# A transformer block in split fp32: q, k and dv scratch with one stride per partition and spilled by ScalarE, modulation sums in PSUM, part of the FFN modulation loaded later

## The chip, the core and the metric

The kernel runs on one core of a Trainium2 chip. A core has a matmul engine (TensorE, PE in the profile, with its weight loads as PEld), three engines for elementwise work (VectorE or DVE, ScalarE or ACT, GpSimd or POOL), a fifth that here only issues DMAs (SyncE or SP), and 16 DMA engines that all queues share. Each engine works through its own list of instructions in order and waits on semaphores for the others. The metric is the device time of one execution in microseconds (us); less is better.

## The reference, cut to what matters

One block of a transformer on S = 1024 tokens of width D = 1024, batch 1, depth 1, in float32. A vector `c` modulates both halves of the block through six vectors of 1024 numbers:

```python
c_act = jax.nn.silu(c)
mod = c_act @ w_ada[l] + b_ada[l]                    # [1, 6144]
sh_a, sc_a, g_a, sh_f, sc_f, g_f = jnp.split(mod[:, None, :], 6, axis=-1)
h = rms_norm(x, g_mix[l]) * (1.0 + sc_a) + sh_a
x = x + g_a * hybrid_mixer(h, w_in[l], ...)
h = rms_norm(x, g_ffn[l]) * (1.0 + sc_f) + sh_f
x = x + g_f * swiglu(h, w_ffn_gate[l], w_ffn_up[l], w_ffn_down[l])
return rms_norm(x, g_final)
```

The mixer multiplies `h` by `w_in` (1024 x 2240) and splits the result into `dq` and `dk` (4 heads of 2 x 64 features each), `dv` (4 x 128), `q_lat` (384), `kv_lat` (256) and `k_rope` (64). Four heads are differential attention (two softmaxes with a linear position bias, the second subtracted with a factor lambda), four are latent attention (`q_lat` and `kv_lat` normalised, multiplied up, rotated). Both are causal. Then comes the output projection, and a gated FFN of width 2816.

The six sections of `w_ada` (4 MB each) have the numbers 0 to 5 in the kernel: 0 and 1 (`sh_a`, `sc_a`) are needed before the first matmul of the block, 2 (`g_a`) at the output projection, 3 and 4 (`sh_f`, `sc_f`) at the second norm, 5 (`g_f`) where the FFN's down projection is scaled.

## The kernel before

**Numbers in two parts.** Every fp32 matrix is split into a high and a low part (`split`, L151 and L155: a rounded copy, by ScalarE as a rule, then the difference, by VectorE or GpSimd), and each product is three matmuls (`mm3`, L370 to L372: high by high, high by low, low by high).

**Memory.** All large tiles come from one pool of 49 slots of 4 KB per partition. PSUM has two double banks (`psd`) and four single ones (`psb`). What does not fit goes to scratch in DRAM and comes back (`scr_q`, `scr_k`, `scr_dv`, `scr_mv` and others). SyncE issues all loads (`ld`), GpSimd all spills (`sd`).

**Order.** The code is written as one list of steps, and a scheduler lays the instructions out for each engine from it; instructions marked `pin` keep their place in the written order. `Stream` (L58 to L95) holds the loads with their preparation. `add` appends a pair (DMA, preparation), `allow` sets how far the stream may run, `need` runs it up to a named item, `pump(n)` runs n preparations, and loads are issued up to `ahead` items in front of the preparations. `defer(n, fn)` puts a spill off by n calls of `tick()`.

**Stages.** After the first loads comes

1. `g1(0)`, then `g1(1)` (L414): for one half of the tokens, `dq` and `dk`, transposed (features on the partitions). For each of 8 row tiles k of `w_in`, `make_h` (L353) transposes the normalised x by four matmuls against the identity (L356), ScalarE scales it by the modulation columns into a tile `ht` (L361), and `split` makes `hh` and `hl`. Six outputs are accumulated over k while k runs, two more afterwards. `evac_qk` (L397) splits each of the 8 outputs into a tile E, [128, 2 (high, low), 512], and spills it.
2. During `g1(0)`, `ada_cols(k)` (L217) makes the columns of sections 0 and 1 for row tile k: 8 multiply-add steps on VectorE over weight rows (256 wide, two running sums in SBUF, added at the end), then two matmuls by ones (L229), which add over the partitions, and two small operations into `acol`.
3. `dv` for 8 tiles of 128 tokens (`evac_v`, L463), then `lat_q`, `lat_k` and their up projections mixed with the first attention steps ("fill", with `PUMP` preparations and `ALLOW` limits after each piece), then the rest of the attention steps (`step`), the output projection, the FFN chunk by chunk, and the down projection.

**Sections 2 to 5.** `ada_items(sec, ...)` (L264) adds 8 stream items for a section: each loads 512 KB (`adr`) and adds it, times one number per partition, to a sum `acc` [128, 1024] on VectorE (L275 for the first, L277 for the other seven, each depending on the one before). Three ticks later `row_bc` (L287; sections 2 and 5) makes it a row on all partitions by two pinned matmuls and two additions, or `col_sec` (L305; sections 3 and 4) makes it columns by eight pinned matmuls 1 wide. The stream's order is: 8 pairs of ada and `w_in` tiles, x tiles 4 to 7, section 2, section 4, `w_in` for dv, `w_in` for lat_q, section 3, section 5, `w_in` for lat_k, rope, the two up projections. So all four sections are done before lat_q.

**Scratch.** `scr_q` and `scr_k` are [head, half, P, 2, 512], with row l*64 + r for the high (l = 0) or low (l = 1) part of feature r, and 2 for the softmax m. A spill of an E is two DMAs of 256 KB by GpSimd, one each for the high and the low part (L404). `load_t` (L712) reads for each step A (the high half of q, twice, into the two halves of the partitions), Q (the low half, the same) and K (all of k, one DMA). dv is spilled as four DMAs of 256 KB for each two tiles of tokens, in pieces of 512 bytes (L472).

Of the kernel before, what the change touches and what calls it, by code (L numbers as in the profile page):

```python
# [24 lines left out]
ALLOW = [(6, 'rope'), (15, ('qup', 2)), (25, ('kvup', 1)), (34, None)]  # L25
# [4 lines left out]
PUMP = (2, 2)  # L30
# [66 lines left out]
def emit(ctx, tc, a, out, dbg=None, rec=None):  # L97
# [112 lines left out]

    def load_ada(k):
        adar[k] = [slot([4, 256], F32, "ada") for _ in range(2)]
        for q in range(2):
            ld(out=adar[k][q], in_=a["ada_a"][k, :, q * 4:(q + 1) * 4, :])

    def ada_cols(k):
        acc = slot([2, 256], F32, "acc")  # L217
        for kt in range(8):
            src = adar[k][kt // 4][:, kt % 4, :]
            c = cact[:, kt:kt + 1]  # L220
            if kt < 2:
                nc.vector.tensor_scalar(out=acc[:, kt, :], in0=src, scalar1=c, scalar2=None, op0=ALU.mult)
            else:
                nc.vector.scalar_tensor_tensor(out=acc[:, kt % 2, :], in0=src, scalar=c, in1=acc[:, kt % 2, :],
                                               op0=ALU.mult, op1=ALU.add)
        nc.vector.tensor_tensor(out=acc[:, 0, :], in0=acc[:, 0, :], in1=acc[:, 1, :], op=ALU.add)
        ps = psb()
        for s in range(2):
            mm(ps[:, s:s + 1], lhsT=acc[:, 0, s * 128:(s + 1) * 128], rhs=ones[:, 0:1], start=True, stop=True)  # L229
        nc.vector.scalar_tensor_tensor(out=acol[:, 0, k:k + 1], in0=ps[:, 0:1], scalar=b1col(1, k),  # L230
                                       in1=V[:, 56 + k:57 + k], op0=ALU.add, op1=ALU.mult)
        nc.vector.tensor_tensor(out=acol[:, 1, k:k + 1], in0=ps[:, 1:2], in1=bcol(0, k), op=ALU.add)
        del adar[k]
# [17 lines left out]
    load_ada(0)  # L251
    for t in range(4):
        load_x(t)
    st = Stream(3)
    win = a["w_in"]
    for k in range(8):
        st.add(("ada", k), (lambda k=k: load_ada(k)) if k else (lambda: None), lambda k=k: ada_cols(k))
        witem(st, ("s0", k), win[k * P:(k + 1) * P, 0:1024], [1024], nc.gpsimd)
# [5 lines left out]
    def ada_items(sec, done):  # L264
        for kt in range(8):
# [17 lines left out]
            st.add(("ad", sec, kt), dma, prep)  # L283
# [3 lines left out]
    def row_bc(sec):  # L287
# [3 lines left out]

        st.add(("gb", sec), dma, lambda: None)
# [10 lines left out]
        ada_items(sec, done)  # L303

    def col_sec(sec, fin):  # L305
        def done(acc):
            ps = psb()
            for j in range(8):
                pin(mm(ps[:, j:j + 1], lhsT=acc[:, j * 128:(j + 1) * 128], rhs=ones[:, 0:1], start=True, stop=True))
            fin(ps)  # L310

        ada_items(sec, done)
# [7 lines left out]

    row_bc(2)
    col_sec(4, fin_scf)
    for q in range(4):
        witem(st, ("dv", q), win[q * 256:(q + 1) * 256, 1024:1536].rearrange("(k p) n -> p k n", p=P), [2, 512], nc.gpsimd)
    for q in range(4):
        witem(st, ("lq", q), win[q * 256:(q + 1) * 256, 1536:1920].rearrange("(k p) n -> p k n", p=P), [2, 384])
    col_sec(3, fin_shf)
    row_bc(5)

# [3 lines left out]

    for q in range(3):
        n = 3 if q < 2 else 2
        witem(st, ("lk", q), win[q * 384:q * 384 + n * 128, 1920:2240].rearrange("(k p) n -> p k n", p=P), [n, 320])
# [3 lines left out]
    for k in range(2):  # L340
        witem(st, ("kvup", k), a["w_kv_up"][k * P:(k + 1) * P, :], [1024], nc.gpsimd)

# [10 lines left out]
    def make_h(hf, k):  # L353
# [6 lines left out]
        tmp = slot([512], F32, "ht")  # L360
        nc.scalar.activation(tmp, ps, AF.Identity, scale=acol[:, 0, k:k + 1], bias=acol[:, 1, k:k + 1])  # L361
        split(tmp, hi, lo)
# [17 lines left out]
    scratch("q", [4, 2, P, 2, 512])  # L380
    scratch("k", [4, 2, P, 2, 512])
# [14 lines left out]
    def evac_qk(ps, m, hf):  # L396
# [4 lines left out]
        def spill():  # L401
            q = scr["q" if m < 4 else "k"][h, hf].rearrange("(l r) m t -> l m r t", l=2)
            for l in range(2):
                sd(out=q[l], in_=f(E[:, l, :]))  # L404
# [7 lines left out]
    st.load(6)  # L412

    def g1(hf):  # L414
# [3 lines left out]
        def prep(k):  # L418
            if hf == 0:
                st.need(("s0", k))  # L420
            make_h(hf, k)

# [32 lines left out]
    st.allow(("ad", 5, 7))  # L455
# [4 lines left out]
    def evac_v(ps, name, t):  # L460
        if t % 2 == 0:
            vt[name] = (slot([2, 512], F32R, "vh"), slot([2, 512], F32R, "vl"))
        hi, lo = vt[name]  # L463
        evac(ps, 1.0, hi[:, t % 2, :], lo[:, t % 2, :])
# [3 lines left out]
        def spill():  # L468
            for l, z in ((0, hi), (1, lo)):
# [552 lines left out]
    for n in range(done, NS):  # L1022
        step(n, LA)
        if n - NU in WOL:
# [189 lines left out]
    for c in range(NP):  # L1214
        res = {}
        gen = [gu(c, kind, res) for kind in KINDS]
        for w, m in order if c == 0 else [(0, 0)] * 6 + [(1, 0)] * 6:
            next(gen[w])
            more(m)
    A.clear()  # L1220
# [64 lines left out]
```

## Time and profile before

| | |
|---|---|
| runs | 1349.02, 1353.95, 1357.58 us (median 1353.95) |
| the profiled execution, its own time | 1355.32 us |
| its span in the profile | 1353.5 us |
| its mean granted TensorE clock | 0.965 |
| PE busy | 1245.5 us, 92% of the span |
| DVE busy | 843.7 us, 62% |
| POOL busy | 534.8 us, 40% |
| ACT busy | 454.7 us, 34% |
| DMA | 180.61 MB, mean 133 GB/s |

The profile shows one execution. An engine's busy time is the time in which it ran an instruction. It doesn't say whether that instruction was on the path that sets the end. PE is busy nearly throughout, but a busy PE also covers matmuls at a lowered clock or spread out by waits, so a stage has to be held against what its matmuls take when nothing holds them up. Part 2 of the page cuts the span in 40 slices of 33.8 us. The first seven hold the stages before `lat_q`, and there the digits of PE differ most from 9. "Waits" lists, for each instruction, what it waited for last, and the "chain" is followed back from the last instruction to what released each one.

### The profile page before, as it was taken

The numbers are of one execution on the slowest core, as the hardware profiler recorded it, in microseconds if no ns is written. First come the engines' busy times: TensorE is split into PE (matmuls) and PEld (weight loads), VectorE is DVE, ScalarE is ACT, GpSimd is POOL, SyncE is SP. The second block draws the span as 40 slices with busy tenths as digits, with TensorE's granted clock in tenths as the row PEclk, the third lists the DMA queues.
The fourth block names the chain that finished last, engine by engine and source line by source line (L and its number), as shares of the span: only waits on it lengthen the run. The fifth ranks groups of instructions, "written<-read, shape, count | busy, mean of one in ns | idle before, by whom it ended". The sixth has DMA issues, their size and how long they took to land.

```text
span 1353.5 us, 16478 instructions
## 1 busy us (share of the span) xinstructions
PE 1245.5 (92%) x6033; PEld 1041.0 (77%) x6033; DVE 843.7 (62%) x1219; ACT 454.7 (34%) x801; POOL 534.8 (40%) x576
## 2 busy tenths in 40 slices
PE   4795995999999999999889999999999988999996
PEld 3574774898888898887668888888888866887885
DVE  6762426165778887867875545565555689576446
ACT  3241220254566676314632232322232332121002
POOL 3341421236564335412474444455544563221003
PEclk9897896999999999999999999999999989999998
DMA  9537589433687533441021222222221764231003
GB/s 365 198 73 192 184 189 330 141 118 98 214 293 255 172 114 108 154 140 62 32 84 57 94 94 87 84 88 85 93 70 55 247 267 134 68 125 47 0 0 124
DMA packets 66765, 180.61 MB, mean 133 GB/s; under 512 B 20654, under 2 KB 23036, under 8 KB 66556
## 3 DMA queue, kind: packets, MB, share of 16 engines
q1 hardware_dynamic: 40891, 139.58, 30.0%
q0 software_dynamic: 25792, 39.97, 10.1%
q8 instruction: 48, 0.79, 0.2%
q14 instruction: 34, 0.27, 0.1%
HBM read 135.37 MB, written 44.04 MB: 133 GB/s over the span
## 4 chain that ended last, share of the span: by engine, by line
PE 70%; DVE 11%; DMA 7%; issue 5%; ACT 4%; POOL 2%; SPq 0%; POOLq 0%; DVEq 0%; ACTq 0%
PE psb L370 14%; PE psb L371 14%; PE psb L372 14%; PE psd L371 6%; PE psd L370 5%; PE psd L372 5%; PE psb L829 2%; DMA adr<-in_w_ada_dram 2%; DMA scr_q<-E 2%; DMA scr_k<-E 1%; DVE x L1175 1%; DVE wlo L151 1%; PE psb L853 1%; PE psb L854 1%; PE psb L852 1%
## 5 line engine op out<-in xcount | busy, mean ns | idle before, releaser
L371 PE MATMUL psb<-al,whi 128*128 128x512 f32 x528 | 206.8, 392 | 3.5 <-DVE al L151 3.5
L370 PE MATMUL psb<-ah,whi 128*128 128x512 f32 x528 | 206.6, 391 | 0.2 <-ACT ht L1057 0.2
L372 PE MATMUL psb<-ah,wlo 128*128 128x512 f32 x528 | 206.2, 391 | 0.0
L1175 DVE TENSOR_TENSOR x<-psd,x 128x1024 f32<-128x1024 f32 x87 | 105.8, 1220 | 77.5 <-PE psd L372 77.5
L370 PE MATMUL psd<-dhi,whi 128*128 128x512 f32 x348 | 138.1, 397 | 13.0 <-DVE x L1175 12.9
L371 PE MATMUL psd<-dlo,whi 128*128 128x512 f32 x348 | 136.8, 393 | 0.0
L372 PE MATMUL psd<-dhi,wlo 128*128 128x512 f32 x348 | 136.8, 393 | 0.0
L1134 DVE TENSOR_TENSOR cf<-psb,uv 128x512 f32<-128x512 f32 x88 | 60.4, 686 | 115.7 <-PE psb L372 115.1
L1141 POOL TENSOR_TENSOR cf<-cf,cf 128x512 f32<-128x512 f32 x44 | 61.7, 1402 | 178.9 <-DVE cf L1134 173.6
L371 PEld LDWEIGHTS psb<-al,whi 128*128 128x128 f32 x528 | 99.5, 188 | 25.2 <-DVE al L151 4.7
L370 PEld LDWEIGHTS psb<-ah,whi 128*128 128x128 f32 x528 | 99.7, 189 | 21.7 <-ACT ht L1057 0.7
L372 PEld LDWEIGHTS psb<-ah,wlo 128*128 128x128 f32 x528 | 99.6, 189 | 20.8
L639 POOL TENSOR_TENSOR raw<-raw,gbc 128x1024 f32<-128x1024 f32 x26 | 66.9, 2587 | 102.9 <-DVE x L1175 48.8
L151 DVE TENSOR_TENSOR wlo<-raw,whi 128x1024 fp32r<-128x1024 f32 (+3 forms) x51 | 92.7, 1823 | 6.4 <-ACT whi L155 5.0
L155 ACT CAST whi<-ssum 128x1024 fp32r<-128x1024 f32 x44 | 45.0, 1044 | 136.2 <-POOL ssum L151 136.2
L370 PEld LDWEIGHTS psd<-dhi,whi 128*128 128x128 f32 x348 | 66.0, 190 | 30.8 <-DVE x L1175 17.2
L151 DVE TENSOR_TENSOR wlo<-ssum,whi 128x1024 fp32r<-128x1024 f32 x44 | 62.9, 1430 | 39.5 <-ACT whi L155 39.5
L748 ACT ACTIVATE s<-s,nb 128x640 f32<-128x640 f32 (+7 forms) x96 | 74.5, 778 | 34.0 <-DVE nb L746 30.6
L746 DVE CUSTOM_DVE_ANT_0 s<-psd,tabs 128x640 f32<-128x640 f32 (+7 forms) x80 | 63.4, 804 | 32.2 <-PE psd L772 30.3
L155 ACT CAST whi<-raw 128x1024 fp32r<-128x1024 f32 (+3 forms) x68 | 68.5, 1019 | 41.9 <-DVE dlo L151 29.9
L372 PEld LDWEIGHTS psd<-dhi,wlo 128*128 128x128 f32 x348 | 66.0, 190 | 14.2 <-DVE wlo L151 0.3
L371 PEld LDWEIGHTS psd<-dlo,whi 128*128 128x128 f32 x348 | 66.2, 190 | 13.6
(290 smaller groups left out, 2958.5 us busy)
## 6 DMA issues: line engine op xcount, KB each, us to landing
adr<-in_w_ada_dram SPq DMA_DIRECT2D x32, 512.0 KB, 10.5
raw<-in_w_gate_dram SPq DMA_DIRECT2D x22, 512.0 KB, 4.4
raw<-in_w_up_dram SPq DMA_DIRECT2D x22, 512.0 KB, 3.4
scr_g<-cf POOLq DMA_DIRECT2D x22, 512.0 KB, 4.4
raw<-in_w_down_dram SPq DMA_DIRECT2D x22, 512.0 KB, 4.3
raw<-scr_g SPq DMA_DIRECT2D x22, 512.0 KB, 4.6
ada<-in_ada_a_dram SPq DMA_DIRECT2D x16, 512.0 KB, 10.2
x<-in_x_dram SPq DMA_DIRECT2D x16, 512.0 KB, 5.1
```

What stands on the lines that cost most here:

```text
L151: eng.tensor_tensor(out=o, in0=x, in1=y, op=ALU.subtract)
L155: nc.scalar.copy(hi, raw)
L370: mm(o, lhsT=ah, rhs=bh, start=start, stop=False)
L371: mm(o, lhsT=ah, rhs=bl, start=False, stop=False)
L372: mm(o, lhsT=al, rhs=bh, start=False, stop=stop)
L639: eng.tensor_tensor(out=r, in0=r, in1=gbc[sec], op=ALU.mult)
L746: nc.vector.tensor_tensor_reduce(out=s, in0=src, in1=tab, op0=ALU.add, op1=ALU.min, scale=scale, scalar=3.0e38, accum_out=nb[:, m:m + 1])
L748: nc.scalar.activation(s, s, AF.Exp, bias=nb[:, m:m + 1], scale=-1.0, accum_out=rs[:, m:m + 1])
L829: nc.tensor.transpose(ps[:, z * 128:(z + 1) * 128], p[:, kb * 128:(kb + 1) * 128], ident)
L1134: nc.vector.tensor_tensor(out=o, in0=x, in1=y, op=ALU.add)
L1141: nc.gpsimd.tensor_tensor(out=g, in0=g, in1=o, op=ALU.mult)
L1175: nc.vector.tensor_tensor(out=r, in0=d.rearrange("p a b -> p (a b)"), in1=r, op=ALU.add)
```

## The change

**Scratch and spills.** `scr_q` and `scr_k` become [head, half, 2 (high, low), 2 x 64 features, 512], so that a partition of E goes to rows of one stride, and a spill is one DMA of 512 KB instead of two of 256. ScalarE issues it instead of GpSimd, as it does the spills of dv and mv, which become two DMAs of 512 KB for each two tiles (in pieces of 1 KB) instead of four. Since high and low now lie apart, K too is loaded as two halves of the partitions.

```diff
-    scratch("q", [4, 2, P, 2, 512])
-    scratch("k", [4, 2, P, 2, 512])
+    scratch("q", [4, 2, 2, P, 512])
+    scratch("k", [4, 2, 2, P, 512])
...
         def spill():
-            q = scr["q" if m < 4 else "k"][h, hf].rearrange("(l r) m t -> l m r t", l=2)
-            for l in range(2):
-                sd(out=q[l], in_=f(E[:, l, :]))
+            q = scr["q" if m < 4 else "k"][h, hf].rearrange("l p t -> p l t")
+            nc.scalar.dma_start(out=q, in_=f(E))
...
-                for tt in range(2):
-                    u = t - 1 + tt
-                    sd(out=scr[name][:, u // 4, :, l, u % 4, :].rearrange("h p d -> p h d"),
-                       in_=f(z[:, tt, :]).rearrange("p (h d) -> p h d", h=4))
+                nc.scalar.dma_start(out=scr[name][:, u // 4, :, l, u % 4:u % 4 + 2, :].rearrange("h p t d -> p h (t d)"),
+                                    in_=f(z).rearrange("p h t d -> p h (t d)"))
...
-        if key[0] in "AQ":
-            r = src[0:64] if key[0] == "A" else src[64:128]
+        if key[0] in ("A", "Q", "K"):
             for u in range(2):
-                ld(out=f(t[u * 64:(u + 1) * 64]), in_=r)
+                l = {"A": 0, "Q": 1, "K": u}[key[0]]
+                ld(out=f(t[u * 64:(u + 1) * 64]), in_=src[l].rearrange("(m r) t -> r m t", m=2))
```

On POOL, in the row before (from the last norm of x to the splits of the dv weights), E is a tile of one output and `2x64x512 x2` are its two DMAs:

```order
L204 TENSOR_TENSOR rstd_122_605<-rstd_122_605,mhalf_75 128x1
L404 DMA scr_q_106<-E_125_636 2x64x512 x2
L404 DMA scr_q_106<-E_126_639 2x64x512 x2
L404 DMA scr_q_106<-E_128_644 2x64x512 x2
L404 DMA scr_q_106<-E_130_673 2x64x512 x2
L404 DMA scr_k_107<-E_131_679 2x64x512 x2
L404 DMA scr_k_107<-E_132_685 2x64x512 x2
L404 DMA scr_k_107<-E_133_690 2x64x512 x2
L404 DMA scr_k_107<-E_134_695 2x64x512 x2
L151 TENSOR_TENSOR wlo_181_956<-raw_174_899,whi_180_955 128x1024
```

On ACT, in the row after, at the same place of the program (the end of `g1(0)`; L414 and L417 evacuate an output into E, L385 is the scaling in `make_h` for the first tiles of `g1(1)`):

```order
L417 ACTIVATE E_112_600<-psd_23_151 128x512
L417 ACTIVATE E_114_605<-psd_23_151 128x512
L417 ACTIVATE E_115_609<-psd_24_152 128x512
L427 DMA scr_q_106<-E_112_600 128x2x512
L417 ACTIVATE E_117_638<-psd_24_152 128x512
L414 CAST E_118_643<-psb_25_153 128x512
L427 DMA scr_q_106<-E_114_605 128x2x512
L414 CAST E_119_647<-psb_26_154 128x512
L427 DMA scr_q_106<-E_115_609 128x2x512
L414 CAST E_120_651<-psb_111_575 128x512
L427 DMA scr_q_106<-E_117_638 128x2x512
```

The spills have moved from one run on POOL to places between the evacuations on ACT, each behind two later evacuations.

**Modulation sums in PSUM.** The eight row tiles of sections 0 and 1 are now taken in chunks `CHUNKS` of one or two tiles (256 or 512 columns), whose weights the host lays out for it (`ada_b`). The sum runs in one PSUM bank, its last step goes to an SBUF tile, and three small operations replace two. `make_h` scales in place in PSUM and has no `ht`. The x tiles are loaded before ada 0, the stream looks 5 items ahead from the start, and the first `w_in` tile is split by VectorE.

```diff
+    CHUNKS = {0: 1, 1: 1, 2: 2, 4: 2, 6: 1, 7: 1}
...
+        for kt in range(8):
+            src = adar[k][kt // per][:, kt % per, :]
+            c = cact[:, kt:kt + 1]
+            if kt == 0:
+                nc.vector.tensor_scalar(out=ps[:, 0:w], in0=src, scalar1=c, scalar2=None, op0=ALU.mult)
+            else:
+                nc.vector.scalar_tensor_tensor(out=acc[:, 0:w] if kt == 7 else ps[:, 0:w], in0=src, scalar=c, in1=ps[:, 0:w],
+                                               op0=ALU.mult, op1=ALU.add)
...
-    load_ada(0)
     for t in range(4):
         load_x(t)
-    st = Stream(3)
+    load_ada(0)
+    st = Stream(5)
...
-        tmp = slot([512], F32, "ht")
-        nc.scalar.activation(tmp, ps, AF.Identity, scale=acol[:, 0, k:k + 1], bias=acol[:, 1, k:k + 1])
-        split(tmp, hi, lo)
+        nc.scalar.activation(ps, ps, AF.Identity, scale=acol[:, 0, k:k + 1], bias=acol[:, 1, k:k + 1])
+        split(ps, hi, lo)
```

On DVE, in the row before, from the norm of the last of the first four x tiles (L349) on; the first `hl` is what the first matmuls of `g1(0)` need, and `acc_42` is the sum for row tile 1:

```order
L349 TENSOR_SCALAR x_8_104<-x_8_104,rstd_22_152 128x1024
L151 TENSOR_TENSOR hl_40_188<-ht_41_189,hh_39_187 128x512
L222 TENSOR_SCALAR acc_42_193<-ada_24_158,cact_81 128x256 x2
L224 SCALAR_TENSOR_TENSOR acc_42_193<-ada_24_158,cact_81,acc_42_193 128x256 x2
L224 SCALAR_TENSOR_TENSOR acc_42_193<-ada_25_159,cact_81,acc_42_193 128x256 x4
L226 TENSOR_TENSOR acc_42_193<-acc_42_193 128x256
```

On DVE, in the row after, from the same norm (L374) on; `psb_42` is the sum for row tile 1, `psb_52` that for tiles 2 and 3:

```order
L374 TENSOR_SCALAR x_6_100<-x_6_100,rstd_22_147 128x1024
L151 TENSOR_TENSOR wlo_29_163<-raw_27_160,whi_28_162 128x1024
L238 TENSOR_SCALAR psb_42_194<-ada_30_166,cact_81 128x256
L240 SCALAR_TENSOR_TENSOR psb_42_194<-ada_30_166,cact_81,psb_42_194 128x256 x3
L240 SCALAR_TENSOR_TENSOR psb_42_194<-ada_31_167,cact_81,psb_42_194 128x256 x3
L238 TENSOR_SCALAR psb_52_231<-ada_33_172,cact_81 128x512
L240 SCALAR_TENSOR_TENSOR psb_52_231<-ada_33_172,cact_81,psb_52_231 128x512
L240 SCALAR_TENSOR_TENSOR psb_52_231<-ada_34_173,cact_81,psb_52_231 128x512 x2
L240 SCALAR_TENSOR_TENSOR psb_52_231<-ada_35_174,cact_81,psb_52_231 128x512 x2
L240 SCALAR_TENSOR_TENSOR psb_52_231<-ada_36_175,cact_81,psb_52_231 128x512
L151 TENSOR_TENSOR hl_41_190<-psb_39_184,hh_40_189 128x512
```

The first `hl` now stands behind the first weight split and behind seven of the eight steps of two sums, the second of which reads four more loads.

**Later loads.** Section 4 goes behind the dv weights. Section 3 leaves the stream and gets one of its own, pumped once for each attention step after the fill. Section 5 goes into the FFN's stream, two items for each chunk from the second on. `row_bc` and `col_sec` now return their items, and the bias row is loaded in the place before the last two weights. `PUMP` and `ALLOW` in the fill are changed to go with it, and the FFN loop calls `tick()`.

```diff
-ALLOW = [(6, 'rope'), (15, ('qup', 2)), (25, ('kvup', 1)), (34, None)]
+ALLOW = [(0, 'rope'), (12, ('qup', 2)), (25, None)]
-PUMP = (2, 2)
+PUMP = (1, 1)
...
+    st3 = Stream(2)
+    for it in col_sec(3, fin_shf):
+        st3.add(*it)
...
+    late_ada = row_bc(5)
...
+        if c >= 1:
+            for _ in range(2):
+                if late_ada:
+                    st2.add(*late_ada.pop(0))
...
         step(n, LA)
+        if n > done:
+            st3.allow()
+            st3.pump()
```

More of the change, by code (lines that the diff above doesn't have):

```diff
@@ L209, in emit @@
     W = {}
+    CHUNKS = {0: 1, 1: 1, 2: 2, 4: 2, 6: 1, 7: 1}
     def load_ada(k):
-        adar[k] = [slot([4, 256], F32, "ada") for _ in range(2)]
-        for q in range(2):
-            ld(out=adar[k][q], in_=a["ada_a"][k, :, q * 4:(q + 1) * 4, :])
-    def ada_cols(k):
[L217 to L233, printed above, removed]
@@ new lines, in load_ada, with ada_src, ada_sum @@
+        n = CHUNKS[k]
+        src = ada_src(k)
+        per = 4 // n
+        adar[k] = [slot([per, 256 * n], F32, "ada") for _ in range(2 * n)]
+        for q in range(2 * n):
+            ld(out=adar[k][q], in_=src[:, q * per:(q + 1) * per, :])
+    def ada_src(k):
+        if CHUNKS[k] == 2:
+            return a["ada_b"][k // 2 - 1]
+        return a["ada_a"][k if k < 2 else k - 4]
+    adac = {}
+    def ada_sum(k):
+        n = CHUNKS[k]
+        w = 256 * n
+        per = 4 // n
+        ps = psb()
+        acc = slot([512], F32, "acc")
+        for kt in range(8):
[6 more added lines that the diff above has]
+                                               op0=ALU.mult, op1=ALU.add)
+        del adar[k]
+        adac[k] = (ps, acc)
@@ new lines, in ada_cols @@
+    def ada_cols(k):
+        n = CHUNKS[k]
+        ps, acc = adac.pop(k)
+        for s in range(2 * n):
+            mm(ps[:, s:s + 1], lhsT=acc[:, s * 128:(s + 1) * 128], rhs=ones[:, 0:1], start=True, stop=True)
+        sc = ps[:, 0:2 * n].rearrange("p (k s) -> p s k", s=2)
+        ac = acol[:, 0, k:k + n]
+        nc.vector.tensor_tensor(out=ac, in0=sc[:, 0, :], in1=V1[:, 8 + k:8 + k + n], op=ALU.add)
+        nc.vector.tensor_tensor(out=ac, in0=ac, in1=V[:, 56 + k:56 + k + n], op=ALU.mult)
+        nc.vector.tensor_tensor(out=acol[:, 1, k:k + n], in0=sc[:, 1, :], in1=V[:, 8 + k:8 + k + n], op=ALU.add)
@@ L249, in witem @@
         st.add(name, dma, prep)
-    load_ada(0)
     for t in range(4):
         load_x(t)
-    st = Stream(3)
+    load_ada(0)
+    st = Stream(5)
     win = a["w_in"]
-    for k in range(8):
-        st.add(("ada", k), (lambda k=k: load_ada(k)) if k else (lambda: None), lambda k=k: ada_cols(k))
-        witem(st, ("s0", k), win[k * P:(k + 1) * P, 0:1024], [1024], nc.gpsimd)
+    for k, n in CHUNKS.items():
+        st.add(("ada", k), (lambda k=k: load_ada(k)) if k else (lambda: None), lambda k=k: ada_sum(k))
+        for k in range(k, k + n):
+            witem(st, ("s0", k), win[k * P:(k + 1) * P, 0:1024], [1024], nc.gpsimd if k else nc.vector)
     for t in range(4, 8):
@@ L264, in ada_items @@
     def ada_items(sec, done):
+        its = []
         for kt in range(8):
@@ L281, in prep @@
                     defer(3, lambda: done(acc))
-            st.add(("ad", sec, kt), dma, prep)
+            its.append((("ad", sec, kt), dma, prep))
+        return its
     gbc = {}
@@ L332, in load_tabs @@
         ld(out=raws["rope"], in_=a["rope"])
+    for it in row_bc(2):
+        st.add(*it)
+    for q in range(4):
+        witem(st, ("dv", q), win[q * 256:(q + 1) * 256, 1024:1536].rearrange("(k p) n -> p k n", p=P), [2, 512], nc.gpsimd)
+    for it in col_sec(4, fin_scf):
+        st.add(*it)
+    for q in range(4):
+        witem(st, ("lq", q), win[q * 256:(q + 1) * 256, 1536:1920].rearrange("(k p) n -> p k n", p=P), [2, 384])
     for q in range(3):
@@ L419, in prep @@
             if hf == 0:
+                if k in CHUNKS:
+                    st.need(("ada", k))
+                    ada_cols(k)
                 st.need(("s0", k))
             make_h(hf, k)
+            if hf == 0 and k and k + 1 in CHUNKS:
+                st.need(("ada", k + 1))
         prep(0)
```

29 lines of the change are left out of this document (12 added, 17 removed).

## The prediction

> **What bounds the kernel now.** I read part 2 of the page first: where is PE not at 9?
>
> ```profile
> PE   4795995999999999999889999999999988999996
> ```
>
> Seven slices of 33.8 us at the start hold most of the lost time. The windows view prices the stages. After us its columns are PE, PEld, DVE, ACT, POOL busy (instructions), the granted clock, the DMA engines' busy share and GB/s.
>
> ```profile
> 20.00:95.30 75.30, 63.08 (x248) 48.61 (x249) 56.30 (x99) 23.93 (x37) 29.47 (x23) 0.86 0.52 184
> 95.30:158.50 63.20, 46.26 (x195) 37.03 (x194) 23.28 (x26) 17.55 (x25) 15.85 (x13) 0.84 0.70 202
> 158.50:245.30 86.80, 67.45 (x266) 53.53 (x265) 34.33 (x45) 11.26 (x18) 23.97 (x32) 0.82 0.85 249
> 410.00:450.00 40.00, 38.16 (x274) 35.13 (x274) 33.09 (x93) 27.71 (x70) 16.02 (x37) 1.00 0.66 225
> 450.00:610.00 160.00, 157.60 (x971) 139.36 (x970) 122.35 (x248) 77.78 (x166) 59.16 (x79) 1.00 0.42 135
> 690.00:1090.00 400.00, 400.00 (x1765) 330.89 (x1763) 225.51 (x237) 113.74 (x149) 205.89 (x148) 1.00 0.29 101
> ```
>
> The first three are `g1(0)`, most of `g1(1)`, and its rest with dv: 225.3 us. What would they take unhindered? Two ScalarE rows of the timeline bracket one dv tile, which is 24 matmuls 512 wide, and a PE row has 8 transposes:
>
> ```profile
> 238.12 0.59 ACT L390 CAST vh<-psb 128x512 fp32r<-128x512 f32 x1 [4.85 <-PE psb L372]
> 243.56 0.58 ACT L390 CAST vh<-psb 128x512 fp32r<-128x512 f32 x1 [4.86 <-PE psb L372]
> 95.30 1.03 PE L356 MATMUL psb<-ident,x 128*128 128x128 f32 x8
> ```
>
> 5.44 us, so 0.227 us for a matmul. A half of g1 has 192 of them (43.5 us) and 32 transposes (4 x 1.03 = 4.1), 47.6 in all; dv has 8 x 5.44 = 43.5. The floor is 47.6 + 47.6 + 43.5 = 139 us, and 86 us are lost. The waits and the chain say to what (chain: start, us, what was waited for or ran):
>
> ```profile
> PE psd L371 <- DVE hl L151: 18.0, 6, 9.2
> PE psb L229 <- DVE acc L226: 13.6, 5, 8.3
> POOL scr_k L404 <- DMA scr_q<-E: 31.4, 12, 8.4
> ACT E L390 <- DMA scr_q<-E: 26.1, 3, 12.1
> ACT ht L361 <- DMA scr_k<-E: 19.3, 1, 19.3
> ...
> 88.40 3.19 POOL scr_q L404 x4
> 91.58 22.55 DMA scr_q<-E
> 114.66 19.21 DMA scr_k<-E
> 163.05 2.49 PE psb L309 x16
> 189.56 16.49 DMA adr<-in_w_ada_dram
> 208.68 9.69 DMA adr<-in_w_ada_dram
> 243.53 1.72 PE psb L299 x4
> ```
>
> Three causes. In `g1(0)` PE waits for `hl` and for the modulation sums. After it the spills hold E, and so the slots and ScalarE: 22.6 + 19.2 us of the chain. In dv it is the modulation weights: 16.5 + 9.7 us.
>
> **Part 1, the spills.** The DMA issues give KB each and the median from issue to landing:
>
> ```profile
> scr_q<-E POOLq DMA_DIRECT2D x16, 256.0 KB, 17.6
> scr_k<-E POOLq DMA_DIRECT2D x16, 256.0 KB, 21.2
> scr_qn<-E POOLq DMA_DIRECT2D x6, 512.0 KB, 4.2
> op<-scr_q SPq DMA_DIRECT2D x32, 256.0 KB, 4.8
> op<-scr_k SPq DMA_DIRECT2D x12, 512.0 KB, 5.9
> ```
>
> The new spill has no row of its own. The nearest is `scr_qn`: the same tile E, the same 512 KB, one DMA with the partitions outermost, 4.2 us. The other bound is the old pace, 17.6 and more, if crowding and not the pattern makes the spills slow. I take something near 4.2, up to 10 in a crowd. Then the 41.8 us of the chain go, and what is late next is the modulation weights and PE itself.
>
> The Trainium skill's page "DMA: Bandwidth & Descriptors" says under "Why a DMA increments its semaphore by 16 and not by 1" that a DMA is spread over the largest number up to 16 that divides the outermost sizes of both sides; the old pattern's outermost size is 2, the new one's 128. By that the old spill ran on 2 engines, and 4.2 would be right; the sum below is 1313 by it and 1333 if the pattern does nothing. The same page, under "Issuing engines are not separate DMA queues", speaks against the queue's part: a move to another issuer saves only issue time; by this nothing of the 41.8 would come from ScalarE's queue alone, which leads to the time of the third rival.
>
> K in two halves: 12 more loads, 5.9 us each before, 4.8 for a half. They are issued five items ahead, so I take 0; uncovered it would be 12 x one issue, and the issue is 0.33 (rows in part 2), 4 us. The Trainium skill's page "DMA: Bandwidth & Descriptors" speaks against this part in its "Rules for kernel authors": two transfers to disjoint halves of the partitions share the same engines, and one over all 128 is to be used. The trace points the same way (4.8 for 256 KB, 5.9 for 512), and by that rule the sum would be up to 4 us above mine.
>
> ScalarE gets 16 q and k spills and 16 for dv and mv, 32 x 0.33 = 11 us of issue, against an ACT that is busy 53 of the 225 us. Hidden too; POOL loses its 0.80 apiece (3.19 for 4). What queues behind such a spill on ScalarE is two evacuations later, and those are waited for by PE through their banks: the last rival.
>
> **Part 2, the start and the sums.**
>
> ```profile
> 20.10 0.80 PE L370 MATMUL psd<-hh,whi 128*128 128x512 f32 x1 [1.52 <-ACT hh L155]
> 6.63 2.46 DVE L224 SCALAR_TENSOR_TENSOR acc<-ada,cact,acc 128x256 f32<-128x256 f32 x6
> 21.21 4.57 DVE L224 SCALAR_TENSOR_TENSOR acc<-ada,cact,acc 128x256 f32<-128x256 f32 x6
> 21.07 2.45 POOL L151 TENSOR_TENSOR wlo<-raw,whi 128x1024 fp32r<-128x1024 f32 x1 [3.57 <-ACT whi L155]
> 29.70 2.81 DVE L151 TENSOR_TENSOR hl<-ht,hh 128x512 fp32r<-128x512 f32 x1
> 6.10 0.62 DVE L222 TENSOR_SCALAR acc<-ada,cact 128x256 f32<-128x256 f32 x2 [1.91 <-DMA ada<-in_ada_a_dram]
> 13.76 0.75 DVE L349 TENSOR_SCALAR x<-x,rstd 128x1024 f32<-128x1024 f32 x1 [0.52 <-POOL rstd L204]
> 22.93 0.33 SPq L240 DMA_DIRECT2D raw<-in_w_in_dram  x1
> 30.65 0.33 SPq L240 DMA_DIRECT2D raw<-in_w_in_dram  x1
> L866 DVE SCALAR_TENSOR_TENSOR mg<-psb,g,mg 128x256 fp32r<-128x256 f32 x16 | 7.7, 480 | 1.6 <-ACT mg L865 1.5
> L965 DVE SCALAR_TENSOR_TENSOR x<-psb,rsd,x 128x512 f32<-128x512 f32 x64 | 43.0, 742 | 3.0 <-PE psb L372 3.0
> L151 DVE TENSOR_TENSOR wlo<-ssum,whi 128x1024 fp32r<-128x1024 f32 x44 | 62.9, 1430 | 39.5 <-ACT whi L155 39.5
> L277 DVE SCALAR_TENSOR_TENSOR acc<-adr,cact,acc 128x1024 f32<-128x1024 f32 x28 | 35.9, 1282 | 18.9 <-DMA adr<-in_w_ada_dram 18.5
> ```
>
> Six sum steps take 2.46 us alone and 4.57 beside a GpSimd split of 2.45: VectorE stood still about 2.1 us. `hl` takes 2.81 there. The same operations with one operand in PSUM (L866, L965) run at 0.48 and 0.74 on average, among much other GpSimd work, so I take them as undisturbed. No row writes such a result to PSUM; bounds are 0.41 (2.46 / 6) and 0.75 a step, and I take 0.50 for 256 columns and 0.77 for 512, the PSUM rows with a little added.
>
> The price is at the start. The SP rows have six DMAs of 512 KB between them in 7.72 us, so one lands each 1.29 us. Ada 0 landed its first half at 6.1 before; behind four x tiles its second half lands at 6.1 + 5 x 1.29 = 12.5. By the order, VectorE then has the last four of its sum steps (2.0), the columns (an estimate of 1.5: two small products of PE, three steps smaller than any here), four norms (4 x 0.75), the first weight split (1.4), seven steps of 256 (3.5), seven of 512 (5.4) and the first `hl` (0.7, as an L965 step): 12.5 + 2.0 + 1.5 + 3.0 + 1.4 + 3.5 + 5.4 + 0.7 = 30. With the matmuls' start and some waits I put PE's first at 32 instead of 20.1. From there the port holds nothing, and two tiles' columns come at once: g1(0) ends near 90 (32 + 47.6 + some 10 of waits) instead of 95.3. I take 5 us gained, between -4 (19 us of waits stay) and 12 (3 stay).
>
> Then g1(1), 47.6 and 4 for section 2's pinned products (1.72) and waits: 142. dv 43.5: 186. Section 4's pinned products (2.49, the L309 row) and waits for its weights, 8 loads in a stage that had 16 before: lat_q starts between 190 and 197 instead of 245.3; I take 194, a gain of 51.
>
> **Part 3, what comes later.** Section 3: 8 sums on VectorE, 8 x 1.28 = 10.3 us, and 2.49 of pinned products, in attention, where from 410 to 450 VectorE is busy 33.1 of 40. It has 7 free, so 3.3 of the 10.3 can't be hidden there. Later (122 of 160) they can. Bounds 3 and 12.8; I take 7, half way, since each sum holds the in-order VectorE for 1.3 us. Section 5: 10.3 us of VectorE in the FFN, where it is busy 226 of 400 and PE 400 of 400. Hidden if it doesn't stop the operation that frees PE's bank. Its two bank-wide fp32 products are on PE: 1.72. Bounds 1.7 and 12.7 (each sum in the way, the products, 0.7 for an addition); I take 3.5, near the lower, since PE there waits for nothing. POOL's 206 of 400 gets nothing new.
>
> **The sum.** 1353.5 - 51 + 7 + 3.5 = 1313 for the span. The profiled run's own time is 1.8 above its span and 1.4 above the median of the three, 1353.95, so the span and 0.4 is the forecast: 1313.
>
> **The rivals.** (1) The stages come nearer to their floor and the later work is covered: lat_q at 190 (-55), given back 3 + 1.7. 1353.5 - 55 + 4.7 + 0.4 = 1304. For it: POOL's spills and the port blocking go at once. Against it: PE's late start.
>
> (2) The later loads cost more: sections 3 and 5 wholly in the way, 12.8 + 12.7 = 25.5 instead of 10.5: 1328. For it: VectorE at 83% from 410 to 450, and one queue (SP) in which a load that waits for a slot holds all behind it. Against it: PE is the bound in the FFN with VectorE a little over half busy.
>
> (3) Change without the effect: the spills are slow because loads crowd them (the DMA engines are 0.70 busy from 95 to 158), and stay at 17 to 21 us. Then only g1(0)'s 5 and the weights' 16.5 + 9.7 are gained, 31, less 10.5: 1353.5 - 31.2 + 10.5 + 0.4 = 1333. Against it: `scr_qn` at 4.2, though in emptier stages.
>
> (4) Slower: ScalarE, in order, stands at each spill until VectorE has written the low part, which stands behind one sum (1.28) and one evacuation (0.7). 32 x 2 = 64 us, all on PE's path: 1313 + 64 = 1377. It decides for slower than before from 41 / 32 = 1.3 us a spill. Against it: each spill stands two evacuations late, and the sums lie mostly elsewhere.
>
> **How the numbers follow.** The forecast has 0.58, (1) 0.16, (2) 0.13, (3) 0.08, (4) 0.05. The range goes from 1296, case (1) with the 7 us more that g1(0) gains at its own bound, to 1334, which takes in (2) and (3); case (4) and the tails of the others are the 2 in 10 left out. One per cent is 13.5 us, about what a measurement of this kernel can tell from no change: faster is below 1340.4. All but (4) lie there; (3) lies 7 from the line. So faster 0.91, same 0.05, slower 0.04.
>
> **What would show it.** In the profile after: scr_q and scr_k at 512 KB with 4 to 10 us to landing (at 17, case 3); the first L370 near 32; g1(0) ending near 90; no step of DVE at twice its length beside POOL; the first lat_q matmuls near 194; PE short of 9 in the slices past 410 if case 2; ACT idle before its spills, released by DVE, if case 4. It is wrong if the stages before lat_q still take 220 us, or if the attention grows by more than 12.

## The result, and the profile after

| | before | after |
|---|---|---|
| median, us | 1353.36 (4 runs, 1349.02 to 1357.58) | 1320.78 (4 runs, 1316.03 to 1321.92) |
| ratio, 95% interval | | 0.9753 [0.9714, 0.9792] |
| span of the profiled execution, us | 1353.5 | 1319.2 |
| mean granted TensorE clock | 0.965 | 0.987 |

The kernel is 2.5% faster, 33 us, where 41 were forecast. One execution of a kernel below, the one with the spill part alone, took 2046.58 us at a granted clock of 0.56 instead of 0.98, and no comparison uses it. Part 2 of the page of the kernel after shows where PE filled up (slices of 33 us):

```profile
PE   1899999999989999998899999999999988999996
```

Before, the digits were 4795995. The view by windows gives the stages up to `lat_q`: from just before the first product with `hl` to the end of `g1(0)`, then `g1(1)`, then dv. Columns are us, then PE, PEld, DVE, ACT and POOL busy (instructions), the granted clock, the DMA engines' share, and GB/s.

```profile
30.00:92.00 62.00, 55.23 (x244) 44.91 (x245) 35.05 (x67) 23.36 (x36) 20.98 (x15) 0.97 0.45 167
92.00:142.00 50.00, 47.29 (x217) 37.58 (x216) 16.84 (x22) 18.46 (x28) 9.46 (x4) 1.00 0.58 210
142.00:190.00 48.00, 48.00 (x221) 40.03 (x220) 21.91 (x31) 11.95 (x17) 0.00 (x0) 1.00 0.86 288
```

`g1(1)` and dv, which took about 150 us from 95.3 to 245.3, take 98, near their floor of 91, and at a granted clock of 1.00 instead of 0.82 to 0.84. The DMA issues of the kernel after have the spills (KB each, median us from issue to landing):

```profile
adr<-in_w_ada_dram SPq DMA_DIRECT2D x32, 512.0 KB, 6.0
...
op<-scr_k SPq DMA_DIRECT2D x24, 256.0 KB, 4.5
...
scr_q<-E ACTq DMA_DIRECT2D x8, 512.0 KB, 3.4
scr_k<-E ACTq DMA_DIRECT2D x8, 512.0 KB, 9.0
```

Twice the bytes land in a fifth to a half of the time. The loads of the modulation weights, 10.5 before, also land in 6.0.

Fixed points of the two traces, and of the kernel before with only the spill part of the change (an experiment below), say how the gain builds up and shrinks again. They are starts of instructions that all three have, in us; the last columns are the gain against before. `vh` is the high part of a tile of dv, `latq` a tile of `q_lat`, `mg` the output of an attention block, `cf` a tile of the FFN's gated product.

| | before | after | spill part alone | gain, after | gain, spill part |
|---|---|---|---|---|---|
| first product with `hl` | 20.8 | 32.9 | 20.8 | -12.1 | 0.0 |
| first E of `g1(0)` | 84.6 | 80.5 | 84.6 | 4.1 | 0.0 |
| first E of `g1(1)` | 152.0 | 128.1 | 131.0 | 23.9 | 21.0 |
| first `vh` of dv | 195.8 | 150.3 | 157.3 | 45.5 | 38.5 |
| first `latq` | 249.5 | 194.4 | 204.6 | 55.1 | 44.9 |
| `mg` of the ninth last block of differential attention, on ScalarE | 407.1 | 356.0 | 366.7 | 51.1 | 40.4 |
| the next `mg` | 413.7 | 361.7 | 372.4 | 52.0 | 41.3 |
| the last of these `mg` | 524.9 | 486.0 | 488.6 | 38.9 | 36.3 |
| first `cf` of the FFN | 672.6 | 633.6 | 636.2 | 39.0 | 36.4 |
| last `cf` | 1084.6 | 1048.9 | 1047.9 | 35.7 | 36.7 |
| end | 1353.5 | 1319.2 | 1318.2 | 34.3 | 35.3 |

So 55 us were gained before `lat_q`, 13 were given back between 362 and 486 us, and 3.3 in the FFN. The last row is the surprise: the rest of the change, ahead by 10 us at `lat_q`, has nothing left of it at the end.

Where the 13 go, the windows view shows. First the kernel before, from the `mg` at 413.7 in three pieces, then the kernel after from its own at 361.7:

```profile
413.50:431.20 17.70, 17.11 (x128) 16.05 (x128) 13.67 (x40) 12.09 (x30) 8.51 (x22) 1.00 0.85 282
431.20:467.30 36.10, 34.84 (x241) 31.50 (x240) 30.26 (x76) 25.75 (x60) 12.78 (x25) 1.00 0.52 165
467.30:486.20 18.90, 18.90 (x138) 17.56 (x137) 16.22 (x42) 12.85 (x32) 6.24 (x13) 1.00 0.39 135
```

```profile
361.50:388.00 26.50, 21.42 (x132) 18.22 (x131) 22.14 (x48) 12.87 (x32) 12.32 (x20) 0.94 1.04 331
388.00:425.30 37.30, 36.86 (x252) 33.86 (x253) 30.31 (x77) 25.48 (x60) 12.91 (x27) 0.95 0.54 161
425.30:447.30 22.00, 20.70 (x138) 18.97 (x137) 16.30 (x42) 12.78 (x33) 6.29 (x13) 0.92 0.47 149
```

The first piece takes 8.8 us more (section 3's loads and sums are in it: the DMA engines are full, and VectorE has 22.1 us of work instead of 13.7), the second 1.2, and the third 3.1. No work was added to the third: PE has the same 138 instructions. The clock is below 1.00 in all three.

### The profile page after: what moved, and what is told of

Read it like the earlier page. It is cut to its first block, busy times and chain, and to the rows that moved or that the text cites. A ratio compares the mean times of both kernels' runs of the same rounds, so it can differ in the third digit from the quotient of the medians.

```text
span 1319.2 us, 16325 instructions
## 1 busy us (share of the span) xinstructions
PE 1231.8 (93%) x6033; PEld 1032.1 (78%) x6033; DVE 829.4 (63%) x1198; ACT 453.5 (34%) x801; POOL 491.0 (37%) x511
## 4 chain that ended last, share of the span: by engine, by line
PE 75%; DVE 11%; issue 4%; ACT 4%; DMA 3%; POOL 1%; SPq 0%; ACTq 0%; POOLq 0%; DVEq 0%
PE psb L394 16%; PE psb L396 15%; PE psb L395 15%; PE psd L394 7%; PE psd L395 7%; PE psd L396 7%; DVE wlo L151 2%; PE psb L859 1%; DVE x L1208 1%; ACT s L778 1%; DMA adr<-in_w_ada_dram 1%; DVE al L151 1%; PE psb L883 1%; PE psb L884 1%; PE psb L882 1%
## 5 line engine op out<-in xcount | busy, mean ns | idle before, releaser
L1174 POOL TENSOR_TENSOR cf<-cf,cf 128x512 f32<-128x512 f32 x44 | 65.7, 1492 | 179.0 <-DVE cf L1167 173.5
```

What stands on the lines that cost most here:

```text
L1174: nc.gpsimd.tensor_tensor(out=g, in0=g, in1=o, op=ALU.mult)
```

## The experiments

First the price of section 3 in the attention, then the spills and the sums, each by itself, then both edits together. Every time below is a median, with its ratio to runs of the kernel before on the same chip.

**Section 3: loads, sums or place?** Three edits of the kernel after.

```diff
 loads only
-                    nc.vector.scalar_tensor_tensor(out=accs[sec], in0=src, scalar=c, in1=accs[sec],
+                    w = 16 if sec == 3 else 1024
+                    nc.vector.scalar_tensor_tensor(out=accs[sec][:, 0:w], in0=src[:, 0:w], scalar=c, in1=accs[sec][:, 0:w],
 sums only
+                if sec == 3 and kt:
+                    return
...
-                src = raws.pop(("ad", sec, kt))
+                src = raws[("ad", sec, 0)] if sec == 3 else raws.pop(("ad", sec, kt))
 14 steps later
-        if n > done:
+        if n > done + 14:
```

> The changed kernel, but of section 3's sums only the first is made over all 1024 columns; the other seven run over 16 columns, so that part of the modulation is left out. All 8 loads of 512 KB stay where they are. VectorE loses about 7 x 1.2 = 8 us of work between 360 and 385 us. If the transfers cost the time (section 3's 4 MB fill the DMA engines and the loads of q and k come late), the attention still gives back 10 to 13 us and the time stays at 1317 to 1321. If it is VectorE's in-order work, most of it comes back: 1308 to 1312.

Measured 1314.03 us, 0.9684 [0.9655, 0.9713].

> The changed kernel, but of section 3 only the first 512 KB are loaded, and all eight sums read that tile, so seven eighths of that section's weights are left out. VectorE's work stays. If the transfers cost the time, the attention gives back 3 us or less in place of 13 and the time is 1308 to 1312. If it is VectorE's work, it stays at 1318 to 1322.

Measured 1318.04 us, 0.9719 [0.9681, 0.9757].

The traces are sharper here than the times: the kernel after and the four of this part have one and the same order on PE up to `lat_q` and yet reach it between 191.3 and 196.2 us, so a stretch behind it says more than the end. From the `mg` at 361.7 to the last one it is 111.2 us in the kernel before, 124.3 after, 120.7 with loads only, and 122.7 with sums only. Each theory expected to find nearly all of the 13 us; taking away the sums gets back 3.6 and taking away the loads 1.6. Neither theory holds alone, and some of the 13 us is not section 3's. How far one execution can be trusted here is told by two pairs of kernels below that have one order on PE from `lat_q` on: the kernel after and the one with small chunks take 124.3 us both, but the two with the spills on GpSimd and section 3 at this place take 120.4 and 122.8. So 2.4 us can be scatter, and the 1.6 show nothing.

> The changed kernel with section 3's eight items 14 attention steps later, at about 430 to 465 us, where the DMA engines are busy 0.2 to 0.6 instead of 1.0. If the transfers cost the time, 8 to 10 us come back: 1310 to 1313. If VectorE's work costs it, there is less to get, since VectorE is still busy 16 to 17 of 20 us there: 1315 to 1319.

Measured 1327.00 us, 0.9780 [0.9750, 0.9810]: later is no faster than the kernel after, against both theories, and by the trace it is slower. The same stretch takes 130.7 us. A timeline of VectorE there (start, us, instruction):

```profile
433.17 1.21 DVE L776 CUSTOM_DVE_ANT_0 s<-psd,tabs 128x1024 f32<-128x1024 f32 x1
434.31 0.08 DVE L776 DVE_READ_ACCUMULATOR2_ANT nb<- 128x1 f32 x1
434.31 1.22 DVE L776 CUSTOM_DVE_ANT_0 s<-psd,tabs 128x1024 f32<-128x1024 f32 x1
435.45 0.08 DVE L776 DVE_READ_ACCUMULATOR2_ANT nb<- 128x1 f32 x1
435.45 0.69 DVE L151 TENSOR_TENSOR ptl<-psb,pth 128x512 fp32r<-128x512 f32 x1
436.06 1.28 DVE L300 SCALAR_TENSOR_TENSOR acc<-adr,cact,acc 128x1024 f32<-128x1024 f32 x1
437.25 0.16 DVE L829 RECIPROCAL rr<-rs 128x2 f32<-128x2 f32 x1
437.44 0.27 DVE L831 TENSOR_SCALAR nb<-rs,rr,neglam 128x1 f32<-128x1 f32 x1
```

The sum (L300) stands in front of the reciprocal and the factor (L829, L831) on which the block's probabilities wait, with VectorE working without a pause. PE waits behind it. The windows view of this kernel there:

```profile
430.00:455.00 25.00, 21.11 (x118) 19.58 (x117) 17.07 (x43) 12.31 (x29) 4.28 (x11) 0.80 0.46 151
```

PE is busy 21.1 of 25 us, and the granted clock is 0.80. The chain of that stretch (start, us, instruction):

```profile
443.75 3.20 PE psb L332 x16
...
447.91 0.43 PE psd L817
```

A matmul 512 wide takes 0.43 us instead of 0.23, and the 16 pinned ones of section 3 take 3.20, where they are 1.84 in the chain of the kernel after. It would be natural to charge the half pace to the sum, but the kernel after has it at the same place (window 425 to 447) with no sum near:

```profile
440.30 0.43 PE psd L817
```

The piece takes 25.7 us here against 22.0 in the kernel after, and these 3.7 us are less than the sum's 1.28 and the pinned matmuls' 3.20 together. Over the whole stretch section 3 costs 14.6 us at this place (130.7 against 116.1 in the kernel with the spill part alone, below). Its sums take 10.7 us of VectorE and its pinned matmuls 3.2, so here nearly all of its work stands in the way, and no more than that is shown.

> As the kernel with section 3 later, and section 5 right behind it in the attention steps instead of the FFN. If section 5 costs the FFN 3.3 us by its place there (the difference of the two traces), the FFN gets them back and the attention pays 1.7 us of PE for the two products: 1308 to 1312, 1 to 3 us below the kernel with only section 3 later. If the 3.3 are the work itself wherever it stands, it is equal to that kernel within 1 us; if the attention has no room left on VectorE, it is slower than that kernel by 3 or more.

Section 5 follows section 3 in the attention's stream, with the same later start. Measured 1328.28 us, 0.9805 [0.9767, 0.9843]. The FFN (first to last `cf`) falls from 415.3 to 411.2 us, and was 412.0 before: section 5 costs 3.3 to 4.1 us there. The attention pays it back and more, with 136.4 us for the stretch that took 130.7, and 150.2 instead of 147.6 from there to the first `cf`.

**The spills.** The spill part alone, put into the kernel before; then, in the kernel after, the old layout with its two DMAs but by ScalarE, and the new layout by GpSimd.

```diff
 old layout, ScalarE
+            q = scr["q" if m < 4 else "k"][h, hf].rearrange("(l r) m t -> l m r t", l=2)
+            for l in range(2):
+                nc.scalar.dma_start(out=q[l], in_=f(E[:, l, :]))
 new layout, GpSimd (the same for dv and mv)
-            nc.scalar.dma_start(out=q, in_=f(E))
+            sd(out=q, in_=f(E))
```

> The kernel before with the spills and scratch of the change alone (rows of one stride, one DMA of 512 KB, ScalarE's queue, dv and mv in pieces of 1 KB, K in two halves); start, sums and the order of the sections as before. If the spills were the 41.8 us of the chain, g1(1) ends some 25 to 35 us earlier, and the waits for the modulation weights in dv keep the rest: the time is 1318 to 1330. If crowding and not the pattern made them slow, they still take 15 us or more to land and the time is above 1345.

Measured 1317.86 us (3 runs), 0.9759 [0.9715, 0.9804]: as much as the whole change. One more run has the profile.

> The kernel before with the spill part of the change alone, once more for its profile (its time was 1319.6). The chain up to lat_q should hold no scr_q or scr_k spill, g1(0) should start at 20 and end at 95 us as before, the two waits for modulation weights in dv (16.5 and 9.7 us) should still be there or be longer, and the attention, with no section 3 in it, should take as long as before or 3 us more (K in two halves). The gain of some 33 us should stand in g1(1) and dv.

One run, 1319.95 us. `g1(0)` is as before, and the gain stands in `g1(1)` and dv. But the waits for modulation weights in dv, expected to stay, are gone. Its loads `adr` land sooner from 95 to 206 us:

```profile
adr<-in_w_ada_dram SPq DMA_DIRECT2D x26, 512.0 KB, 6.1
```

No sum waits for one there, and the chain of that stretch holds none. (One evacuation of a `vh` has 8.4 us of ScalarE's idle time put down to an `adr`, off the chain.) Of the attention's 13 us, 4.9 (116.1 against 111.2) are in this kernel, with no section 3 in its attention.

> The changed kernel with the old layout of q and k and two DMAs of 256 KB for each E, issued by ScalarE; K in one load again; dv and mv stay changed. If the pattern makes the spills slow, they land in 15 us or more from ScalarE's queue as well, and the time is 1335 to 1355. If GpSimd's queue made them slow, they land in under 8 us and the time is 1318 to 1323.

Measured 1434.70 us, 1.0617 [1.0559, 1.0676]: far worse than either theory had it. The windows view of this kernel, in a stretch in which only the spills move:

```profile
106.00:116.00 10.00, 0.00 (x0) 0.00 (x0) 0.69 (x1) 0.59 (x1) 0.00 (x0) 0.50 0.13 51
```

0.13 of 16 engines is two, at 51 GB/s. The chain shows the price on ScalarE:

```profile
252.61 5.63 ACTq L428
258.33 23.73 DMA scr_k<-E
```

Issuing alone takes ScalarE 3.4 to 7.5 us (median 6.2) for each of the 16 DMAs of k and 0.5 to 5.0 (median 4.8) for each of q, where one DMA of the new layout takes 0.37, and ScalarE runs nothing meanwhile. In the kernel before, the same pattern by GpSimd looked otherwise (DMA queues from 80 to 140 us: packets, MB, share of 16 engines):

```profile
q0 software_dynamic: 8448, 4.25, 36.9%
```

That is 503 bytes a packet (4.25 MB by 8448). It isn't two engines either: in the window 92 to 100 us this queue alone takes 69.7% of the time of all 16.

```profile
q0 software_dynamic: 1931, 1.16, 69.7%
```

With the old layout, so, both queues are slow, each in its own way.

> The changed kernel with the new layout and sizes, but all q, k, dv and mv spills issued by GpSimd as before. If the pattern is the cause, they land in 4 to 9 us and the time stays within 4 us of the changed kernel, 1317 to 1325. If the queue is the cause, they land in 14 us or more and the time is above 1335.

Measured 1314.09 us (2 runs), 0.9725 [0.9669, 0.9781]. The spills land fast from GpSimd's queue too:

```profile
scr_q<-E POOLq DMA_DIRECT2D x8, 512.0 KB, 5.6
scr_k<-E POOLq DMA_DIRECT2D x8, 512.0 KB, 8.9
```

So the layout was the cause, with the one DMA instead of two that it allows (no kernel here separates these two), and ScalarE's queue no part of the gain. In the window 75 to 100 us q0 has this row, 3.7 KB a packet:

```profile
q0 software_dynamic: 1063, 3.90, 39.4%
```

**The sums.** Chunks of one row tile throughout.

```diff
-    CHUNKS = {0: 1, 1: 1, 2: 2, 4: 2, 6: 1, 7: 1}
+    CHUNKS = {k: 1 for k in range(8)}
```

> The changed kernel with all sums for sections 0 and 1 in chunks of one row tile (256 columns), still in PSUM. If VectorE's steps for the chunk of two ahead of the first low part make PE start late (32.9 us by the trace), PE's first product of that kind comes 3 to 5 us earlier. Whether the end of g1(0), at about 92 us, moves tells if that start cost anything: if the start is on the path, the time is 3 to 5 us lower, 1314 to 1318; if later sums bound g1(0) anyway (16 more small steps on VectorE), it is 1319 to 1325.

Measured 1310.92 us (1305.41 to 1316.18), 0.9688 [0.9641, 0.9735]. The first `hl` product comes only 1.7 us earlier (31.2), the first E of `g1(0)` 5.9 earlier (74.6), 2.8 below the earliest of those five kernels with the old chunks. The four kernels with small chunks in this document have it at 73.2 to 74.6, the six with the old ones and the new spills' layout at 77.4 to 80.7. In time the gain is not shown: the interval overlaps that of the kernel after. The sums of one tile let the columns come one by one. The waits from 32 to 80 us (engine, line and what it waited for: us, times, longest), of the kernel after:

```profile
ACT psb L385 <- DVE acol L253: 36.2, 5, 12.3
```

and of this one:

```profile
ACT psb L383 <- DVE acol L251: 27.3, 6, 9.5
```

ScalarE's scaling waits for a chunk's columns up to 12.3 us, and with small chunks up to 9.5. Of the gain up to the first E, 1.7 us are the start, and the rest is put down to such waits, with some 3 us of scatter in it.

**Together.** Both edits; then, with them, section 3 in the output projection; then section 3 at every fifth step.

```diff
 output projection, the pump in the attention steps taken out
     for t in range(8):
+        if t < 4:
+            st3.allow()
+            st3.pump(2)
+        if t == 3:
+            flush()
 every fifth step
-        if n > done:
+        if n > done and (n - done) % 5 == 1:
```

> The changed kernel with the spills issued by GpSimd again (new layout and sizes kept) and with the sums of sections 0 and 1 in chunks of one row tile. One look at each alone gave 1314.1 and 1310.9 against 1320.8. If the two gains are separate (GpSimd's issue frees ScalarE in the attention around 350 us, the chunks move g1(0)), they add: 1303 to 1309. If both numbers were scatter of one and the same kernel time, or meet in the same wait, 1311 to 1318.

Measured 1309.03 us, 0.9658 [0.9634, 0.9682]. This is the upper end of what the two gains give together, and its interval overlaps with that of each alone, so the sum is likely and not shown.

> As the kernel with both, and section 3 not in the attention steps but in the output projection, two items for each of its first four row tiles, where TensorE is at its full pace with few waits on VectorE. If section 3's sums and loads cost the attention 8 to 10 us by their place there, these come back: 8 to 10 us below the kernel with both, 1294 to 1301. If the output projection has no room for 10.3 us of VectorE either, or the loads come late for the second norm, it is equal or slower.

Measured 1302.92 us, 0.9616 [0.9596, 0.9635], the fastest kernel here: 18 us below the kernel after, 52 below the one before. The two intervals of this kernel and the one with section 3 in the attention only touch. In the traces the stretch from the ninth last `mg`'s successor to the last takes 116.5 us against 122.8, and between there and the first `cf` 2.9 of the 6.3 us are paid again (150.5 against 147.6). So it is a gain of 3 to 6 us, less than the 8 to 10 that were expected.

> As the kernel with both, with section 3's items at every fifth attention step instead of every one. If it is a crowd (of loads at 350 to 388 us, or of sums close together) that costs the time, it is 5 to 9 us below the kernel with both. If each sum costs the chain its 1.28 us wherever it stands in the attention, it is within 3 us of it, or slower, as the kernel with section 3 fourteen steps later was (1327.0).

Measured 1306.69 us, 0.9648 [0.9619, 0.9676]: within 3 us of the kernel with both, as the theory has it by which the price is each sum's place, not the crowd. The stretch takes 119.8 us against 122.8, but the order that took 122.8 has also taken 120.4, so it is not shown that the crowd has a part in the price.

## Why the prediction came out as it did

**Right in sign, size and range.** 1313 was forecast and 1320.78 measured. 51 us were forecast up to `lat_q`, 55.1 came; 3.5 to be given back in the FFN, 3.3 were. The attention is another matter: the prediction said that it is wrong if the attention grows by more than 12 us, and it grew by 13.1. That the total is only 8 us off owes something to luck, since 4 us more than forecast were gained up to `lat_q` and hide part of it.

**The start.** VectorE's order and the rows gave the first `hl` at 30 and, with some waits, PE's start at 32. The first product with `hl` is at 32.9, with `g1(0)` 4.1 us ahead where 5 were said. The sign named for it, the first high-by-high product (L370), was the wrong one: that one starts at 22.5, and PE then stands 9.1 us for `hl`. The sum itself came out 2.8 us short, 2.3 of which is a wait of VectorE for ScalarE's rounded copy of the first weight tile, which the sum had no term for except its "some waits". The new steps take what was taken from the neighbouring rows (0.50 and 0.77 were written down). By-form groups of VectorE in the kernel after:

```profile
L240 DVE SCALAR_TENSOR_TENSOR psb<-ada,cact,psb 128x256 f32<-128x256 f32 x24 | 11.7, 489 | 0.8
L240 DVE SCALAR_TENSOR_TENSOR psb<-ada,cact,psb 128x512 f32<-128x512 f32 x12 | 9.1, 756 | 0.4
```

**The spills.** "Something near 4.2, up to 10 in a crowd": 3.4 and 9.0. That the pattern and not the crowd or the queue makes them slow is shown by the two kernels that separate layout and queue. The Trainium skill's page "DMA: Bandwidth & Descriptors", in "Why a DMA increments its semaphore by 16 and not by 1", has a pattern with an outermost size of 2 on two engines, and notes as an exception that some copies from GpSimd's queue use all 16. On ScalarE's queue the trace shows the two (0.13 of 16). On GpSimd's, the queue of the kernel before, it doesn't (0.37 of 16 for that queue alone, 0.70 from 92 to 100 us). There the forecast left the exception out and was right by luck: the old spill was slow in another way, in half-kilobyte packets.

**The third cause fell.** The prediction had the waits for modulation weights in dv (16.5 + 9.7 us) as a cause of their own, to be ended by moving sections 3 and 5 away. With the spill part alone, and these sections where they were, they are gone. They were the spills' work too: loads that shared the DMA engines with spills of q, k and dv in small packets (before, from 186 to 222 us, GpSimd's queue had 38.8% of the engines' time, and `adr` took 10.8 us to land). For the forecast it made no difference, because both causes went. For the understanding it does: the spill part alone has all of the 33 us (0.9759 against 0.9753, each to about 0.4%). Of the 10.2 us by which the kernel after is ahead of it at `lat_q`, 4.1 are `g1(0)`'s, and some 6 are left for moving the sections, in one execution of each and with the 5 us of scatter told above. Against these 6 stand the 8.2 us of section 3 in the attention and the 3.3 of section 5 in the FFN. So by these traces the later loads, as a part by themselves, paid for nothing.

**The term that was mis-sized: what the attention gives back.** 7 us were put down and 13.1 measured (124.3 - 111.2), just past the upper bound of 12.8. Section 3 costs 8.2 of them (124.3 - 116.1, against the kernel with only the spill part), close to the 7; other pairs of kernels give 6.0 (117.2 with the old layout by ScalarE, against 111.2 before) and 3.9 to 6.3 (120.4 and 122.8, against 116.5 with section 3 in the output projection). It is not the 3.3 of missing VectorE time alone that makes it. The same work cost 14.6 us fourteen steps later, so its place counts; how much of it the sums' places in VectorE's order and the crowd of loads have each is not shown. The other 4.9 come with the new layout, which had been put at 0 for K's halves. With the old layout (and K in one load) the third piece, 18.9 us before, takes 19.0, and 22.0 to 22.1 in the kernel after, in the one with the spill part alone and with the spills on GpSimd. PE's work there is the same, in another order. In the kernel after, the order on PE at that place is this (`psb_872` is a product of probabilities and values, `psd_868` the scores of a latent block):

```
L859 MATMUL psb_869_4250<-ident_71,s_822_4038 128x128 x3
L882 MATMUL psb_872_4259<-pth_825_4044,op_671_3461 128x256
L883 MATMUL psb_872_4259<-ptl_826_4045,op_671_3461 128x256
L884 MATMUL psb_872_4259<-pth_825_4044,op_671_3461 128x256
...
L859 MATMUL psb_877_4278<-ident_71,s_834_4073 128x128 x4
L817 MATMUL psd_868_4237<-op_644_3347,op_768_3832 128x512
```

With the old layout the ten score matmuls stand fourteen rows earlier, behind the second matmul of the product (the kernel before has them there too):

```
L860 MATMUL psb_869_4254<-ident_71,s_822_4044 128x128 x3
L883 MATMUL psb_872_4263<-pth_825_4050,op_671_3469 128x256
L884 MATMUL psb_872_4263<-ptl_826_4051,op_671_3469 128x256
L818 MATMUL psd_868_4241<-op_644_3355,op_768_3838 128x512
```

Where the scores come later, the softmax that hangs on them does too. The kernel after has PE busy 20.7 of 22.0 us at a clock of 0.92 there, against 18.9 of 18.9 at 1.00. The loads that differ make the scheduler lay PE's work out differently; no load is waited for. All kernels with the new layout have the scores late, both with the old one early, so the order goes with the time, but no run changes the order by itself. Whether it is K's halves or q's new rows, both of which change with the layout, no kernel here separates.

**The rivals.** "Nearer to the floor" (1304) was right up to `lat_q` (55) and wrong behind it. "The later loads cost more" was not borne out: sections 3 and 5 cost 8.2 + 3.3, near the 10.5 of the forecast and far from the 25.5 of the rival, and what the attention lost beyond that came from the layout. "Change without the effect" is out by the spills' landing times. ScalarE's blocking is seen only with the old layout (up to 7.5 us an issue, 82 us slower than before); that spills on ScalarE cost a few us with the new one as well is what 1314.09 with GpSimd's queue suggests, and two runs don't show it.

**The sum, term by term.** Up to `lat_q` -55.1 for -51; to the end of the attention +16.2 (55.1 to 38.9), of which 3 come before 362 us, in the mixed stage of projections and first steps, where nothing had been put down; FFN +3.3 for +3.5; the rest +1.4. Together -34.2 (the spans differ by 34.3), for -40.5.

## What to carry to other kernels

A spill's layout belongs to its price: look at the share of the DMA engines and the bytes a packet, not at the time to landing alone, and when a load is late ask first who shares the engines with it. In a stage where one in-order engine feeds the matmul engine, moved work can cost more than that engine's free time suggests (here 8.2 us at one place and 14.6 at another, where free time could hide all but 3.3), so try it in a stage with slack (here the output projection). Test each part of a change by itself, for one part may carry all of the gain and another pay for nothing.

## What the runs showed of the hardware

- The same spill pattern was slow in two ways: by ScalarE's queue on 2 of 16 DMA engines (share 0.13, 51 GB/s) with 0.5 to 7.5 us of ScalarE for each issue, by GpSimd's in packets of 503 bytes, with up to 69.7% of the time of all 16 engines. With the partitions' rows at one stride GpSimd's queue moved 3.7 KB a packet.
- VectorE's multiply-add from PSUM into PSUM took 0.489 us for 256 columns and 0.756 for 512, like the one from PSUM into SBUF (0.479 and 0.744).
- In stretches in which PE had to wait, some of its matmuls took twice as long: 0.43 us for 512 columns instead of 0.23, at a granted clock of 0.92 over 22 us in the kernel after and of 0.80 over 25 us in the one with section 3 later. In the three stages before `lat_q` the granted clock was 0.82 to 0.86 before and 0.97 to 1.00 after. PE's idle time in them fell from 48.5 to 9.5 us, and its busy time fell as well, from 176.8 to 150.5, of which only some 4 are the pinned products that moved. So the waits taken away there gave more than themselves.
